# A two-layer decoder trunk on one core: the second layer's compressed keys and norm steps on other engines, and unread products in TensorE's waits

## Chip, core and metric

One core of a Trainium2 chip runs the whole program. The metric is device time in microseconds (us) of one execution; the time before is a median of three runs, 762.18 us (760.72 to 763.38). The engines that matter are TensorE (PE in the profile; PEld is its weight load), VectorE (DVE), ScalarE (ACT), GpSimd (POOL), and SyncE (SP), which issues nearly all transfers.

## What is computed

A trunk of two residual layers over 256 tokens of width 1024, all float32. Cut to what matters:

```
h = x
layer 0: mix = dilated sliding-window attention(h)          # 16 heads, three dilations
layer 1: on its way in, once:
           kv = h @ w_kv                                    # six blocks of 256 columns
           k_cmp, v_cmp = compress(kv[0]), compress(kv[1])  # gelu(blocks @ w1 + b1) @ w2 + b2
         q = h @ w_q + b_q; gates = sigmoid(h @ w_gate + b)
         mix = gate0*attn(q, k_cmp, v_cmp) + gate1*attn(q, k_slc, v_slc) + gate2*attn(q, k_win, v_win)
both:    h = layer_norm(ALPHA*h + mix)
         ffn = 16 experts of width 256, two per token (group router, then expert router)
         h = layer_norm(ALPHA*h + ffn)
layer_norm(x) = (x - mean) * rsqrt(var + eps) * g + b
```

## The kernel before

The program is one long stream without loops on the chip. Token chunks are c = 0 and 1, of 128 rows each. Its stages are: attention of layer 0 (0 to 280 us), output projection and router of layer 0 (280 to 313), the sixteen experts of layer 0 in four rounds (313 to 432), the norm between the layers (432 to 447), the shared keys and values and the compressed ones (447 to 530), attention of layer 1 (530 to 620), router (620 to 634), experts (634 to 748) and the last norm (748 to the end).

*Order.* A list scheduler lays out each engine's instructions ahead of time: of the instructions that are ready in its own model of time it takes the one that stands first in the program, and later ones fill holes. On the chip each engine then goes through its list strictly in that order. Blocks under `tc.manual_schedule(engines=PES)` keep TensorE's instructions in the written order. Weight loads are one queue on SP in a written order (`stream`); each waits for a free buffer.

*PSUM banks.* There are eight: two of tag A, two of S, one each of Y, R, T and O. `banks(A="AAYR", ...)` says which tags the uses A, S, T and O go through in turn; `B(use, ...)` takes the next. `banks(A="AA", S="SSY", T="TR", O="O")` at line 969 sets the turns anew at the start of the shared keys and values.

*Projections.* `split` turns a weight block into a high part `wh` (ScalarE, line 251, four pieces of 128x512) and a low part `wl` (subtraction, line 252, VectorE or the engine in `low`). `projT` and `projN` then make 48 products of 256 columns in one bank (`psT_`, `psN_`): 32 read `wh` and 16 read `wl`. `b_q(g)`, g = 0 to 3, makes the queries of layer 1; for g = 1 and 2 the subtractions are GpSimd's. `stack_q` puts the queries in place, with ScalarE casts (lines 313, 314) and VectorE subtractions (315, 316).

*The norm between the layers* (lines 937 to 960). For each chunk: sum of squares on ScalarE (487); z = (x - mean)*g on VectorE (946); `rstd`, nine VectorE instructions on one column (lines 496 to 506: an add, two scalings, three Newton steps of two); z*y + b (950); eight transposes on TensorE (553); then high part, low part and plain copy out of PSUM (955 on ScalarE, 956 on VectorE, 957 on ScalarE). VectorE's list mixes this with the low parts of two weight blocks. The last norm (1220 to 1234) has the same parts, and some of chunk 0's on GpSimd (1228, 1229).

*Compressed keys and values* (1024 to 1082). `hd` is the hidden layer; `hps` transposes it, `hcT` and `hrep` copy it (1059, 1063). Then

```python
    kc_ps = B("O", [64, 64], "kc_ps")          # keys: two products
    V.tensor_scalar(kcs, kc_ps, b2k[0:64], None, op0=ALU.add)
    for half in range(2):
        vc_ps = B("O", [P, 64], "vc_ps")       # values: three products, same single bank O
        S.copy(vcs, vc_ps)
```

so the first `vc_ps` waits until `kcs` has read `kc_ps`. Then come `b_q(1)` and `gx`, the gate logits: products of 48 columns.

*Router* (`Moe.enter`, `route`). Per chunk: transposes, `lt`, copy `ls` (566), `lg`, a chain of small VectorE instructions to `o12` (584), the rank product `rk`, `pos` (849). `moe_round` then gathers rows: `gps`, 32 products of 256 columns plus four with zeros that open the banks (line 655), and the first expert's products `G`.

Of the kernel before, what the change touches and what calls it, by code (L numbers as in the profile page):

```python
# [132 lines left out]
def layers(tc, A, out, pools, keep, general):  # L133
# [23 lines left out]
    def B(use, shape, name):  # L157
        tag = rot[use][turn[use] % len(rot[use])]
        turn[use] += 1
        return psum[tag].tile(shape, F32, tag=tag, name=name)  # L160
# [325 lines left out]
                continue  # L486
            S.activation(junk, r[:, s], AF.Square, bias=nm, scale=1.0, accum_out=q[:, n : n + 1])

    def rstd(q, y):


        n = y.shape[1]
        vh = sm.tile([P, n], F32, tag="vh", name="vh")
        yi = sm.tile([P, n], I32, tag="yi", name="yi")
        t = sm.tile([P, n], F32, tag="yt", name="yt")
        V.tensor_tensor(vh, q[:, :, 0], q[:, :, 1], op=ALU.add)
        V.tensor_scalar(vh, vh, -0.5 / D, -0.5 * EPS, op0=ALU.mult, op1=ALU.add)
        V.tensor_scalar(yi, vh.bitcast(I32), -0.5, 519526879.0, op0=ALU.mult, op1=ALU.add)
        y0 = yi.bitcast(F32)
        for _ in range(3):  # L500
            if n == 1:
                V.scalar_tensor_tensor(t, y0, vh, y0, op0=ALU.mult, op1=ALU.mult)
            else:
                V.tensor_tensor(t, y0, vh, op=ALU.mult)
                V.tensor_tensor(t, t, y0, op=ALU.mult)
            V.scalar_tensor_tensor(y, t, 1.5, y0, op0=ALU.add, op1=ALU.mult)
            y0 = y


    tri = small[:, 1024:1152]  # L510
# [45 lines left out]
    def route(layer, r, q, y, c, cc, o12, sel):  # L556

        wr = wrs[layer]
        rT = pp.tile([P, 8, P], F32, tag="p", name="rT")
        transposeT(r, lambda g, ps: (V.tensor_copy if g == c == 0 else S.copy)(rT[:, 4 * g : 4 * g + 4], ps))  # L560
        lt = B("T", [P, P], "lt")
        for k in range(8):
            b = 32 * (k % 4)
            mm(lt[b : b + 32], wr[:, k], rT[:, k], k < 4, k >= 4)
        ls = kp.tile([P, P], F32, tag="k", name="ls")
        V.tensor_copy(ls, lt)
        lg = B("O", [P, 24], "lg")
        mm(lg, ls, cst("lsel"), True, True)
        rstd(q.unsqueeze(1), y)
        L = mp.tile([P, 24], F32, tag="L", name="L")  # L570
        V.scalar_tensor_tensor(L, lg, y, brs[:, layer], op0=ALU.mult, op1=ALU.add)
        gm = sm.tile([P, 8], F32, tag="gm", name="gm")
        gi = sm.tile([P, 8], U32, tag="gi", name="gi")
        s4 = sm.tile([P, 4], F32, tag="s4", name="s4")
        V.max(gm, L[:, 0:8])
        V.max_index(gi, gm, L[:, 0:8])
        V.tensor_tensor(s4, cst("io16")[:, 0:4], gi[:, 0:1].to_broadcast([P, 4]), op=ALU.not_equal)
        em = mp.tile([P, 16], F32, tag="em", name="em")
        V.scalar_tensor_tensor(em.rearrange("p (g e) -> p g e", g=4), s4.unsqueeze(2).to_broadcast([P, 4, 4]), NEG, L[:, 8:24].rearrange("p (g e) -> p g e", g=4), op0=ALU.mult, op1=ALU.add)
        ev = sm.tile([P, 8], F32, tag="ev", name="ev")  # L580
        ei = sm.tile([P, 8], U32, tag="ei", name="ei")
        V.max(ev, em)
        V.max_index(ei, ev, em)
        V.tensor_tensor(o12, cst("io16").unsqueeze(1).to_broadcast([P, 2, 16]), ei[:, 0:2].unsqueeze(2).to_broadcast([P, 2, 16]), op=ALU.is_equal)
        V.tensor_add(sel, o12[:, 0], o12[:, 1])

        def weights():

            wt = sm.tile([P, 4], F32, tag="wt", name="wt")
            ex = sm.tile([P, 4], F32, tag="ex", name="ex")  # L590
            V.tensor_scalar(wt[:, 0:1], gm[:, 0:1], -1.0, None, op0=ALU.mult)
            S.activation(ex, L[:, 0:4], AF.Exp, bias=wt[:, 0:1], scale=1.0, accum_out=wt[:, 1:2])
            V.tensor_sub(wt[:, 2:3], ev[:, 1:2], ev[:, 0:1])
            S.activation(wt[:, 2:3], wt[:, 2:3], AF.Exp)
            V.scalar_tensor_tensor(wt[:, 1:2], wt[:, 2:3], 1.0, wt[:, 1:2], op0=ALU.add, op1=ALU.mult)
            V.reciprocal(wt[:, 1:2], wt[:, 1:2])
            V.tensor_mul(wt[:, 3:4], wt[:, 2:3], wt[:, 1:2])
            V.tensor_scalar(cc[:, c], o12[:, 0], wt[:, 1:2], None, op0=ALU.mult)
            V.scalar_tensor_tensor(cc[:, c], o12[:, 1], wt[:, 3:4], cc[:, c], op0=ALU.mult, op1=ALU.add)

        return weights
# [17 lines left out]
    def moe_round(layer, hH, hL, r, sums, pos, cc, hook, late, later, rest):  # L619
# [116 lines left out]
        for qd in range(5):  # L736
# [20 lines left out]
            with tc.manual_schedule(engines=PES):  # L757
                if qd:
                    yH = W(1, [P, 2, D], "yH", F32R)
                    yL = W(2, [P, 2, D], "yL", F32R)  # L760
                    down(2 * qd - 2, ha, yH, yL)
                    down(2 * qd - 1, hb, yH, yL)
                    whole[qd - 1] = (ohT, yH, yL)
                if qd < 4:
                    ga = up(2 * qd, xg)
                    if qd == 0:
                        ohT_, cslots_ = places(C)
                    gb_ = up(2 * qd + 1, xg)
                    whole[qd] = (ga, gb_, ohT_, cslots_)
                else:  # L770
                    scatter(3, *whole.pop(3))

    def moe_rest(layer, hH, hL, r, pos, cc):

# [41 lines left out]
    class Moe:  # L816
# [15 lines left out]
        def enter(self, c):  # L832
# [19 lines left out]
            if c == 0:  # L852
                self.low(0, y)
                self.weights[0]()

        def low(self, c, y):
            u, hH, hL = self.u[c], self.hH, self.hL
# [82 lines left out]
    for c in range(2):  # L940
# [4 lines left out]
        for s in halves:  # L945
            V.scalar_tensor_tensor(z[:, s], x[:, c, s], nm, gb[:, 0, s], op0=ALU.add, op1=ALU.mult)
        y = sm.tile([P, 1], F32, tag="y2", name="y2")
        rstd(q.unsqueeze(1), y)
        for s in halves:
            V.scalar_tensor_tensor(z[:, s], z[:, s], y, gb[:, 1, s], op0=ALU.mult, op1=ALU.add)  # L950

# [4 lines left out]
            V.tensor_tensor(dL, src, dH.bitcast(F32), op=ALU.subtract)  # L956
            S.copy(dT, src)

        transposeT(z, evac, "A")
        zs.append(z)  # L960

    for a in range(4):
# [3 lines left out]
    pre["w"] = split(pre["w"])  # L966


    banks(A="AA", S="SSY", T="TR", O="O")
    st["ahead"] = AH3  # L970
    bm = pre["bm"]
    o = [0]
# [70 lines left out]
    qSt = [U([P, 16, P], "qS", F32R) for c in range(2)]  # L1043

    def b_q(g):
        ps = projT(split(take(("wq", g)), low=nc.gpsimd if g in (1, 2) else V), aH, aL)
        for pr in range(2):
            j = 2 * g + pr
            q = kp.tile([P, T], F32, tag="k", name="q")
            S.activation(q, ps[:, pr], AF.Identity, bias=bqs[:, j : j + 1], scale=cst("qs")[:, j : j + 1])  # L1050
            for c in range(2):
                stack_q(qSt[c], j, q[:, c * P : (c + 1) * P])
# [12 lines left out]
    for f in range(2):  # L1065
        mm(kc_ps, w2[:, 0, f], hcT[:, f, 0:64], f == 0, f == 1)
    kcs = sm.tile([64, 64], F32, tag="kcs", name="kcs")
    V.tensor_scalar(kcs, kc_ps, b2k[0:64], None, op0=ALU.add)
    KC = sm.tile([P, 4, 2, 16], F32R, tag="KC", name="KC", bufs=1)
    kcs4 = kcs.rearrange("p (g n) -> p g n", g=4)  # L1070
    for r_ in (lo, hi):
# [3 lines left out]
    for half in range(2):  # L1075
# [4 lines left out]
        vcs = kp.tile([P, 64], F32, tag="k", name="vcs")  # L1080
        S.copy(vcs, vc_ps)
        nc.gpsimd.tensor_tensor(VC[:, 8 * half : 8 * half + 8], vcs.unsqueeze(1).to_broadcast([P, 8, 64]), hm.unsqueeze(2).to_broadcast([P, 8, 64]), op=ALU.mult)
    b_q(1)

    gx = B("T", [P, 2, 48], "gx")
# [134 lines left out]
    for c in range(2):  # L1220
# [7 lines left out]
                nc.gpsimd.tensor_scalar(h2[:, c, s], h[:, c, s], nm, 1.0, op0=ALU.add, op1=ALU.mult)  # L1228
                nc.gpsimd.tensor_tensor(h2[:, c, s], h2[:, c, s], gb[:, 0, s], op=ALU.mult)
        y = sm.tile([P, 1], F32, tag="y", name="y")  # L1230
        rstd(q.unsqueeze(1), y)
        for s, eng in zip(halves, (nc.sync, S)):
            V.scalar_tensor_tensor(h2[:, c, s], h2[:, c, s], y, gb[:, 1, s], op0=ALU.mult, op1=ALU.add)
            eng.dma_start(out[c][:, s], h2[:, c, s])
# [69 lines left out]
```

## Time and profile before

| | |
|---|---|
| median of 3 runs | 762.18 us |
| the profiled execution: its time, its span | 763.41 us, 761.6 us |
| TensorE busy, mean granted clock | 716.1 us (94%), 0.961 of 2.4 GHz |
| VectorE, ScalarE, GpSimd busy | 409.7 us (54%), 319.4 us (42%), 71.4 us (9%) |
| transfers | 166.84 MB, 219 GB/s mean |

A clock of 1.00 is 2.4 GHz and 0.50 is 1.2 GHz; a figure between them is a stretch with some of each. A busy TensorE is not one at its peak: products are pipelined, and at half clock the same busy time holds half the work.

### The profile page before, as it was taken

What the parts mean: (1) busy time and instruction counts of PE and PEld (TensorE: products, weight loads), DVE (VectorE), ACT (ScalarE), POOL (GpSimd) and SP (SyncE); (2) the same over time, 40 slices, a digit from 0 to 9 for tenths busy, and PEclk for the clock granted to TensorE, in tenths of its full rate; (3) what the DMA queues carried; (4) which work ended last, traced back from release to release, by engine and by line L of the source; (5) the groups of instructions that cost most, each with busy time, mean ns of one, the idle gap of its engine ahead of it and who ended that gap; (6) DMA issues with size and microseconds to landing.
All of it is one profiled execution on the core that took longest, in us unless ns stands there. A gap on an engine that the chain in (4) does not pass through costs nothing. (4 is left out here: it accounts for less than half of the span.)

```text
span 761.6 us, 12692 instructions
## 1 busy us (share of the span) xinstructions
PE 716.1 (94%) x4996; PEld 534.2 (70%) x4996; DVE 409.7 (54%) x1066; ACT 319.4 (42%) x709; POOL 71.4 (9%) x107
## 2 busy tenths in 40 slices
PE   8999999999999998999999669979999979999993
PEld 6999999999999976545353369879766635453541
DVE  4664556467455647552341658544885565331426
ACT  5555545555454534131230554434874421321312
POOL 0000000000000001110100002230233221000101
PEclk9999999999999999799999969987999998999997
DMA  7975343434443355589999950103780057798921
GB/s 265 408 279 194 111 166 117 164 123 153 167 166 112 114 219 214 216 341 422 415 416 420 397 168 1 56 1 119 299 357 1 2 188 288 322 413 358 415 114 61
DMA packets 27221, 166.84 MB, mean 219 GB/s; under 512 B 3720, under 2 KB 4232, under 8 KB 9104
## 3 DMA queue, kind: packets, MB, share of 16 engines
q1 hardware_dynamic: 26720, 165.35, 55.3%
q8 instruction: 41, 0.67, 0.4%
q10 hardware_dynamic: 432, 0.59, 0.2%
q14 instruction: 28, 0.23, 0.1%
HBM read 163.83 MB, written 1.05 MB: 216 GB/s over the span
## 5 line engine op out<-in xcount | busy, mean ns | idle before, releaser
L252 DVE TENSOR_TENSOR wl<-w,wh 128x512 fp32r<-128x512 f32 (+1 forms) x123 | 118.1, 993 | 89.3 <-ACT wh L251 71.3
L251 ACT CAST wh<-w 128x512 fp32r<-128x512 f32 (+1 forms) x131 | 104.1, 843 | 87.9 <-issue 15.7
L167 PE MATMUL G<-w,xg 128*64 128x512 f32 x416 | 92.2, 593 | 0.0
L167 PEld LDWEIGHTS G<-w,xg 128*64 128x64 f32 x416 | 29.7, 137 | 58.1 <-issue 55.5
L167 PE MATMUL Y<-wd,hidT 128*64 128x512 f32 x256 | 57.8, 595 | 0.0
L611 DVE SCALAR_TENSOR_TENSOR sil<-sil,G 128x256 f32<-128x256 f32 x16 | 6.7, 420 | 76.1 <-ACT sil L610 76.1
L167 PEld LDWEIGHTS Y<-wd,hidT 128*64 128x64 f32 x256 | 17.8, 137 | 33.7 <-issue 33.3
L176 DVE TENSOR_TENSOR yL<-Y,yH 128x512 fp32r<-128x512 f32 x32 | 22.1, 692 | 32.5 <-ACT yH L175 32.5
L175 ACT CAST yH<-Y 128x512 fp32r<-128x512 f32 x32 | 18.8, 586 | 36.5 <-PE Y L167 36.5
L1150 ACT ACTIVATE p<-p,nmb 128x128 f32<-128x128 f32 (+1 forms) x64 | 28.5, 447 | 10.1 <-DVE nmb L1149 10.1
L616 ACT COPY hidT<-ht 128x256 f32<-128x256 f32 x16 | 6.0, 373 | 63.6 <-PE ht L615 63.6
L167 PE MATMUL gps<-oh,hH 128*128 128x256 f32 x128 | 30.7, 323 | 0.8 <-DVE kept L862 0.8
L167 PE MATMUL mix<-w,obT 128*128 128x512 f32 x64 | 31.1, 601 | 0.0
L167 PE MATMUL gps<-oh,hL 128*128 128x256 f32 x128 | 29.3, 310 | 0.0
L1159 POOL TENSOR_SCALAR p<-p,lb,gates 128x256 f32<-128x256 f32 (+1 forms) x40 | 22.3, 566 | 67.3 <-ACT p L1150 34.4
L610 ACT ACTIVATE sil<-G 128x256 f32<-128x256 f32 x16 | 6.2, 387 | 52.3 <-PE G L167 52.3
L730 DVE SCALAR_TENSOR_TENSOR x<-x,sps 128x512 f32<-128x512 f32 x32 | 21.8, 684 | 11.2 <-PE sps L167 11.0
L167 PE MATMUL sps<-yH,ohT 128*128 128x512 f32 x64 | 25.9, 405 | 0.0
L405 ACT ACTIVATE p<-p,nm 128x384 f32<-128x384 f32 x32 | 19.6, 614 | 14.2 <-DVE nm L404 14.2
L167 PE MATMUL sps<-yL,ohT 128*128 128x512 f32 x64 | 25.3, 396 | 0.0
L167 PEld LDWEIGHTS gps<-oh,hH 128*128 128x128 f32 x128 | 23.7, 225 | 1.8 <-issue 1.5
L648 ACT ACTIVATE xg<-gps,lnT 128x256 f32<-128x256 f32 x32 | 16.1, 562 | 19.5 <-PE gps L167 18.8
(558 smaller groups left out, 1796.7 us busy)
## 6 DMA issues: line engine op xcount, KB each, us to landing
w<-in_gu SPq DMA_DIRECT2D x52, 1024.0 KB, 10.7
w<-in_a_win SPq DMA_DIRECT2D x35, 1024.0 KB, 5.9
wd<-in_dn SPq DMA_DIRECT2D x32, 1024.0 KB, 9.5
wp<-in_gu SPq DMA_DIRECT2D x24, 512.0 KB, 13.2
w<-in_wkv SPq DMA_DIRECT2D x6, 1024.0 KB, 16.6
w<-in_a_wout SPq DMA_DIRECT2D x4, 1024.0 KB, 4.7
w<-in_w SPq DMA_DIRECT2D x4, 1024.0 KB, 19.9
w<-in_wq SPq DMA_DIRECT2D x4, 1024.0 KB, 4.7
```

Source lines behind the costliest of these rows:

```text
L167: nc.tensor.matmul(out, l, r, start=start, stop=stop)
L175: S.copy(dstH, src)
L176: V.tensor_tensor(dstL, src, dstH.bitcast(F32), op=ALU.subtract)
L251: S.copy(h[:, s], w[:, s])
L252: low.tensor_tensor(l[:, s], w[:, s], h[:, s].bitcast(F32), op=ALU.subtract)
L405: S.activation(w, w, AF.Exp, bias=nm, scale=-1.0, accum_out=l)
L610: S.activation(sil[rows], G[:, 0:256], AF.Tanh, scale=0.5)
L611: V.scalar_tensor_tensor(sil[rows], sil[rows], 1.0, G[:, 0:256], op0=ALU.add, op1=ALU.mult)
L648: S.activation(xg[:, k], banks4[k // 2][:, k % 2], AF.Identity, bias=b_, scale=g_)
L730: V.scalar_tensor_tensor(r[:, c, s], r[:, c, s], 1.0 if qd else ALPHA, ps, op0=ALU.mult, op1=ALU.add, accum_out=sums[:, c, n : n + 1])
L1150: S.activation(dst, dst, AF.Exp, bias=nm[:, hl, b : b + 1], scale=-1.0, accum_out=l[:, hl, b : b + 1])
L1159: eng.tensor_scalar(dst, dst, l[:, hl, b : b + 1], gates[:, c, 1 + b, 4 * g + hl : 4 * g + hl + 1], op0=ALU.mult, op1=ALU.mult)
```

## The change

`rstd` takes an engine, and its first Newton instruction becomes a `tensor_scalar` with two column operands; chunk 0 of the norm between the layers and of the last norm gives it GpSimd. A new function `awake` issues products into a bank of use S that nobody reads: 38 of 512 columns after layer 0's last expert products, 9 after chunk 1's transposes in the norm, and in each of both routers two times 6 of 128 columns in float32, on `ls` of chunk 0 and of chunk 1. The transposes of the norm go under manual order. The call of `banks` moves from the start of the shared keys and values to just ahead of `b_q(1)`, so until there the turns of layer 0's experts hold (A="AAYR", S="S", T="T", O="O"). The low parts of `b_q(1)` and `b_q(2)` go to VectorE, and `kcs` to ScalarE.

```diff
-    def rstd(q, y):
+    def rstd(q, y, eng=V):
...
         for _ in range(3):
-            if n == 1:
-                V.scalar_tensor_tensor(t, y0, vh, y0, op0=ALU.mult, op1=ALU.mult)
+            eng.tensor_scalar(t, y0, vh, y0, op0=ALU.mult, op1=ALU.mult)
+            eng.tensor_scalar(y, t, 1.5, y0, op0=ALU.add, op1=ALU.mult)
+            y0 = y
+
+    def awake(n, l=None):
+
+        ps = B("S", [P, 512], "idle")
+        for _ in range(n):
+            if l is None:
+                mm(ps, ones, small[:, 0:512], True, True)
             else:
...
+                mm(ps[:, 0:P], l, l, True, True)
...
         V.tensor_copy(ls, lt)
+        st["ls", c] = ls
...
                     scatter(3, *whole.pop(3))
+                    if layer == 0:
+                        awake(38)
...
                 self.weights[0]()
+            else:
+                for n in range(2):
+                    awake(6, st["ls", n])
...
-        rstd(q.unsqueeze(1), y)
+        rstd(q.unsqueeze(1), y, V if c else nc.gpsimd)
...
-        transposeT(z, evac, "A")
+        with tc.manual_schedule(engines=PES):
+            transposeT(z, evac, "A")
+            if c:
+                awake(9)
...
-    banks(A="AA", S="SSY", T="TR", O="O")
     st["ahead"] = AH3
...
-        ps = projT(split(take(("wq", g)), low=nc.gpsimd if g in (1, 2) else V), aH, aL)
+        ps = projT(split(take(("wq", g))), aH, aL)
...
-    V.tensor_scalar(kcs, kc_ps, b2k[0:64], None, op0=ALU.add)
+    S.activation(kcs, kc_ps, AF.Identity, bias=b2k[0:64], scale=1.0)
...
+    banks(A="AA", S="SSY", T="TR", O="O")
     b_q(1)
...
-        rstd(q.unsqueeze(1), y)
+        rstd(q.unsqueeze(1), y, V if c else nc.gpsimd)
```

## Rows read from the trace of the kernel before

**Rows 1.** TensorE's waits: what waited for what, us in total, times, longest.

```profile
PE hps L553 <- DVE z L950: 9.9, 2, 9.4
...
PE vc_ps L167 <- DVE kcs L1068: 3.8, 1, 3.8
...
PE psT__4818 L167 <- ACT VV L1021: 1.7, 1, 1.7
```

**Rows 2.** Stretches: length, busy and count by engine, TensorE's granted clock, transfers.

```profile
core 0: us, PE busy (x) PEld busy (x) DVE busy (x) ACT busy (x) POOL busy (x), PEclk, DMA share, GB/s
...
302.00:308.00 6.00, 5.04 (x36) 4.50 (x37) 4.11 (x32) 2.13 (x6) 0.61 (x1) 0.55 1.02 427
...
447.00:453.00 6.00, 5.86 (x28) 5.81 (x29) 2.21 (x2) 4.14 (x5) 0.00 (x0) 0.52 0.62 209
...
627.30:633.00 5.70, 5.67 (x25) 5.17 (x25) 4.56 (x12) 0.00 (x0) 1.05 (x1) 0.50 1.01 372
```

**Rows 3.** Timeline of the norm between the layers: start, us, engine, line, operation.

```profile
434.50 0.19 ACT L487 ACTIVATION_READ_ACCUMULATOR junk<-x,nmean 128x1 f32 x1
...
440.86 1.41 DVE L950 SCALAR_TENSOR_TENSOR z<-z,y,lngb 128x512 f32<-128x512 f32 x2
...
447.14 0.58 PE L167 MATMUL psT__4534<-hTH,wh 128*128 128x256 f32 x1 [1.91 <-ACT hTH L955]
```

**Rows 4.** Timeline: runs of like products, with zeros, at full and at half clock.

```profile
297.17 0.81 PE L167 MATMUL gps<-small,zero 1*128 1x512 bf16 x3
...
454.54 2.08 PE L167 MATMUL psT__4534<-hTH,wl 128*128 128x256 f32 x16
...
513.06 3.62 PE L167 MATMUL psT__5104<-hTH,wl 128*128 128x256 f32 x16
```

**Rows 5.** The chain that ended last, 503 to 531 us: start, us, what.

```profile
503.48 1.27 DVE qS L315
...
506.05 0.28 DVE qS L315
...
508.29 1.73 PE vc_ps L167 x6
...
510.96 1.36 PE vc_ps L167 x6
512.32 4.35 PE psT__5104 L167 x19
516.67 5.09 PE gx L167 x36
521.76 8.62 PE psT__5211 L167 x48
```

**Rows 6.** Timeline of GpSimd and ScalarE at the compressed keys.

```profile
500.71 5.16 POOL L252 TENSOR_TENSOR wl<-w,wh 128x512 fp32r<-128x512 f32 x4 [6.25 <-ACT wh L251]
...
503.98 0.30 ACT L314 CAST qS<-q 64x128 fp32r<-64x128 f32 x1
```

**Rows 7.** Two stretches of 1 us in and after the gate logits.

```profile
520.00:521.00 1.00, 1.00 (x11) 1.00 (x10) 0.57 (x2) 0.15 (x1) 0.00 (x0) 1.00 0.02 8
521.00:522.00 1.00, 1.00 (x5) 0.83 (x5) 0.00 (x0) 0.20 (x1) 0.00 (x0) 0.50 0.00 0
```

**Rows 8.** GpSimd's groups by shape: count, busy us, mean ns, idle before.

```profile
L1159 POOL TENSOR_SCALAR p<-p,lb,gates 128x128 f32<-128x128 f32 x16 | 8.1, 515 | 38.9 <-ACT p L1150 27.2 <-DVE nmb L1149 7.1 <-PE ptb L1168 3.0
...
L1294 POOL MEMSET const-float32-0.0<- 128x1 f32 x1 | 0.1, 99 | 0.2 <-issue 0.2
```

**Rows 9.** Timeline of the second router, VectorE.

```profile
627.10 0.17 DVE L849 SCALAR_TENSOR_TENSOR pos<-rk,sel 128x16 f32<-128x16 f32 x1
```

**Rows 10.** The chain that ended last, at the second router.

```profile
627.33 7.13 PE gps L167 x33
```

**Rows 11.** Timeline: the first expert of layer 0.

```profile
313.08 7.09 PE L167 MATMUL G<-w,xg 128*64 128x512 f32 x32
```

**Rows 12.** Timeline of the last norm, GpSimd and VectorE.

```profile
748.62 1.57 POOL L1229 TENSOR_TENSOR h<-h,lngb 128x512 f32<-128x512 f32 x1
...
753.17 1.41 DVE L1233 SCALAR_TENSOR_TENSOR h<-h,y,lngb 128x512 f32<-128x512 f32 x2
```

More of the change, by code (lines that the diff above doesn't have):

```diff
@@ L487, in squares @@
             S.activation(junk, r[:, s], AF.Square, bias=nm, scale=1.0, accum_out=q[:, n : n + 1])
-    def rstd(q, y):
[L492 to L498, printed above, removed]
+    def rstd(q, y, eng=V):
+        vh = sm.tile([P, 1], F32, tag="vh", name="vh")
+        yi = sm.tile([P, 1], I32, tag="yi", name="yi")
+        t = sm.tile([P, 1], F32, tag="yt", name="yt")
+        eng.tensor_tensor(vh, q[:, 0, 0:1], q[:, 0, 1:2], op=ALU.add)
+        eng.tensor_scalar(vh, vh, -0.5 / D, -0.5 * EPS, op0=ALU.mult, op1=ALU.add)
+        eng.tensor_scalar(yi, vh.bitcast(I32), -0.5, 519526879.0, op0=ALU.mult, op1=ALU.add)
         y0 = yi.bitcast(F32)
         for _ in range(3):
-            if n == 1:
-                V.scalar_tensor_tensor(t, y0, vh, y0, op0=ALU.mult, op1=ALU.mult)
-            else:
[L504 to L507, printed above, removed]
+            eng.tensor_scalar(t, y0, vh, y0, op0=ALU.mult, op1=ALU.mult)
[6 more added lines that the diff above has]
+                mm(ps, ones, small[:, 0:512], True, True)
+            else:
+                mm(ps[:, 0:P], l, l, True, True)
     tri = small[:, 1024:1152]
```

## The prediction

> **What bounds the kernel now.** I read the table of engines first: TensorE is busy for 94% of the span, so time can come only from its waits or from its clock. Next its list of waits [rows 1]: three matter here, 9.4 us for the normed rows `z`, 3.8 us of `vc_ps` for `kcs`, and 1.7 us for a free bank. Then the granted clock by stretches [rows 2]: after each long wait the same products go on at 0.50 to 0.55, that is at 1.2 GHz, while the busy column looks full. The price of half clock is in two runs of sixteen like products: 2.08 us at 2.4 GHz and 3.62 us at 1.2 GHz, which is 0.12 us and 0.21 us for each once the last one's own duration is taken off [rows 4]. So a wait is paid twice, as idle time and as slow products behind it. The chain that ended last shows it at its plainest: TensorE idles until 508.29 and works without a hole to 530.38, mostly at half speed [rows 5].
>
> **The change part by part.** The sum is made against the profiled execution, 763.41 us; the median of the runs lies 1.2 us below it.
>
> *The compressed keys.* Before, the wait begins at 508.29 - 3.8 = 504.5, and the last product of `psT__5211` ends at 521.76 + 8.62 = 530.4: 25.9 us [rows 1, 5]. `kcs` came last on VectorE because GpSimd's four subtractions ran from 500.71 to 505.87 [rows 6] and VectorE's subtraction of 64x128 took 1.27 us beside them and 0.28 us after [rows 5]. The Trainium skill's SBUF — State Buffer, section "Who interferes with whom", says that a VectorE instruction with two SBUF inputs and a GpSimd one that reads SBUF block each other fully; by that rule, the trace agrees, 1.27 against 0.28. After, the subtractions are VectorE's: eight more, at most GpSimd's 1.29 us each [rows 6], hidden in VectorE's idle time ahead of the hidden layer and beside TensorE's products; without that cover the four of `b_q(2)` would cost up to 5 us. `kcs` is one ScalarE instruction of about 0.3 us (VectorE's took as much). In front of it stand at worst ScalarE's eight casts, the last of which ends at 504.28 [rows 6], so it ends by 504.6, while TensorE still has 22 products of `psT__5104` to fill the wait. What is left then: 22 at 0.12 = 2.6; the two `vc_ps` groups 3.1 now, between half of that and all, say 2.0; `gx`, 36 products at the 10 to 11 per us that the window at full clock shows [rows 7], 3.4; `psT__5211`. Does the clock hold for it? In the window from 520 `gx` runs at 1.00 with TensorE busy throughout, and from 521 the clock is 0.50, with no idle time between [rows 7]: all that TensorE did ahead of the fall was `gx`. I take that to happen again and leave `psT__5211` at its 8.6. Sum 16.6, and 0.5 for small waits: 17.1, a gain of **8.8 us**. Bounds: 0 if the wait stays, 11.6 if `psT__5211` runs at full clock (48 at 0.12 = 5.8).
>
> *The norm between the layers.* The nine instructions of chunk 0 start at 434.7, when its squares are done, and its `z` came at 440.86 [rows 3]. GpSimd's price for one column has no row; its nearest are 0.10 for a MEMSET of one column and 0.515 for a TENSOR_SCALAR of 128 columns [rows 8]. I take 0.4 to 0.5, near the second, because it is the same operation with column operands: 434.7 + 4 = 438.7 (bounds 435.6 and 439.3). The 38 unread products are 0.21 us each by the distance of the three with zeros [rows 4], 8.1 us. They start when TensorE falls idle, 9.4 us ahead of the first transpose, which follows the first of the two `z` instructions at 441.7 [rows 1, 3], so at 432.3, and end at 440.4: the transposes start 1.3 us earlier and with the clock up. VectorE's list loses nine small instructions and gains dearer forms of others; I cost that at nothing, hidden under its weight subtractions. The first projection began at 447.14 [rows 3], and in 447 to 453 TensorE did 28 products where 50 fit at 0.12 [rows 2]: 2.6 us. Against that stand the nine unread products, 1.9 us, in front of the projection; most of it is hidden, for the last high parts come late from ScalarE's queue of eight copies. Together **2.0 us**, bounds 0 and 3.
>
> *Banks.* With four A banks the 1.7 us wait [rows 1] loses its bank half; the weights of that projection are split in the same queues just then, so I take **0.8 us** of 0 to 1.7.
>
> *Second router.* The 33 gather products take 7.13 us from 627.33 [rows 10], 25 of them in 5.7 us at 0.50 [rows 2]; at 0.12 they take 4.0. The unread products are 24 records, at 0.10 to 0.26 us each (`gx` and `vc_ps` are the nearest), 2.4 to 6.2 us in a stretch with some 3 us idle. A second effect: the last zero product waited for the bank R, held by `rk` until `pos` read it at 627.10 [rows 9, 10]. With `hps` of the hidden layer asked for before `banks` instead of after, the turns of T and R swap by one and `rk` gets T, so chunk 0's gather can start while VectorE works out chunk 1's rank. 3.1 plus 0.4: **3.5 us**, bounds 0 and 4.7.
>
> *First router.* The same at a smaller size: 302 to 308 at 0.55 [rows 2]. Chunk 1's sixteen products would save about 1 us until `G` at 313.08 [rows 11], and `lt` and `lg` ahead of the chain 0.5: **1.5 us**, bounds 0 and 2.5. The transfers of the experts wait there for buffers that `G` frees, so they move along.
>
> *Last norm.* GpSimd's nine instructions stand behind its product that ends at 748.62 + 1.57 = 750.2 [rows 12]; at 0.4 to 0.5 they end near 754.2, when before the output rows started at 753.17. Chunk 1's chain has VectorE to itself meanwhile. I take **0**, bounds 0.7 lost and 0.7 won.
>
> Sum: 8.8 + 2.0 + 0.8 + 3.5 + 1.5 = 16.6. 763.41 - 16.6 = 746.8, and 1.2 lower on the scale of the median: **746 us**. The attention of layer 1, where I see only the same list shifted by one bank, can go 2 us either way.
>
> **The rivals.**
>
> *The clock holds through the gate logits.* With no idle wait ahead of them, `gx` is shorter and has wide products on both sides. Then `psT__5211` gives 2.8 us more: 743. Against it speaks the fall at 521 [rows 7]. The Trainium skill's TensorE: Matmul & The Clock Gate, section "Why this matters for your kernels", asks for no idle gaps between bursts of matmuls; by that rule this would be the likeliest, but the row shows a fall with no gap.
>
> *The fillers are too thin.* Between chunk 0's and chunk 1's transposes TensorE may stand still for 2 to 3 us after the 38, and the routers' fillers come when `ls` is there. If the clock falls all the same, the norm and the first router give nothing and the second 1.0 (its bank): 8.8 + 0.8 + 1.0 = 10.6, 752. For it: in the second router the clock fell after a stretch that was sparse, not empty.
>
> *The wait at the compressed keys moves.* The list may put `kcs` behind casts of the next weights, or the new subtractions ahead of `hrep`; then `vc_ps` waits as long as now, and the change gives 7.8: 754.
>
> *Slower: GpSimd's instructions are dear.* Both chains of nine stand at the head of VectorE's list (`z`, the output rows). At X each, the norm is late by 9X - 6.2 and the end by 9X - 3.0 [rows 3, 12]; 18X - 9.2 exceeds the other 14.6 from X = 1.32 us. The longest GpSimd row shown beside a busy VectorE, 1.57 us but for 512 columns and two inputs [rows 12], would give 19.1 lost: 767. Against: 0.515 for 128 columns, also beside a busy VectorE [rows 8]. By the rule of SBUF — State Buffer cited above (the Trainium skill) each of them could also wait for the VectorE instruction then running; no row here shows that for one column.
>
> **How the numbers follow.** Forecast 0.45; clock holds 0.20; fillers too thin 0.22; wait moves 0.07; slower 0.04; no difference 0.02. The range has to reach from a bit under all good ends (11.6 + 3 + 1.7 + 4.7 + 2.5 + 0.7 = 24.2, 738) to between the last two gains: 738 to 754. 0.3% of this time is 2.3 us, about what can be told from no change. Faster 0.94, same 0.02, slower 0.04.
>
> **What would show it.** In the profile after: no wait of `vc_ps` near 4 us, and `kcs` on ScalarE under 0.4; `gx` at 1.00 and the first half of `psT__5211` at 0.50; 38 products 0.21 apart and transposes at 1.00; first projection at 0.12 a product; the second router's gather starting before its last `pos`, 32 products in about 4 us; GpSimd's nine at 0.4 to 0.5. Wrong it would be if one-column GpSimd work took over 1 us, if the unread products ran 0.43 apart, or if a new wait of several us stood in layer 1's attention.

## The result, and the profile of the changed kernel

The changed kernel takes 753.12 us (median of five runs, 750.46 to 754.13) against 762.18 us for the kernel before: the ratio is 0.987 with a 95% interval from 0.986 to 0.989. It is faster, by 9.1 us where 16 were forecast. The profiled execution is the quickest of the five (750.46 us, span 748.7, mean clock 0.987); the other four have a mean clock of 0.982. Against the profiled execution of before (span 761.6) it gained 12.9 us. Both gaps, from 16 to 12.9 and from 12.9 to 9.1, have to be explained.

I cut the span at five places that every profile shows: the end of layer 0's last expert product, the end of the compressed hidden layer `hd`, the first compressed score `cmp`, the first expert product of layer 1, the end of its last one. Each entry is the length between two of them in us; the fifth stretch, the experts of layer 1, is 114.0 in all but one (114.2 in e4). The runs e1 to e11 are the experiments below.

| kernel | median us | ratio to before | start to last expert product, layer 0 | norm, projections, `hd` | compressed keys | attention, second router | last norm |
|---|---|---|---|---|---|---|---|
| before | 762.18 | | 432.3 | 62.4 | 35.6 | 104.2 | 13.2 |
| changed | 753.12 | 0.987 | 429.8 | 62.5 | 25.6 | 101.0 | 15.8 |
| e1 both norms on VectorE | 749.71 | 0.983 | 431.4 | 61.4 | 27.1 | 101.1 | 13.3 |
| e2 chunk 1's chain first | 746.42 | 0.980 | 429.7 | 58.4 | 27.0 | 101.2 | 13.9 |
| e3 last norm on VectorE | 751.58 | 0.986 | 429.4 | 63.5 | 28.5 | 100.9 | 13.3 |
| e4 no idle products | 757.47 | 0.993 | 432.5 | 64.0 | 28.5 | 102.5 | 15.7 |
| e5 gate logits split | 751.24 | 0.985 | 430.3 | 63.7 | 24.5 | 101.8 | 15.7 |
| e6 best of both | 744.25 | 0.977 | 430.4 | 59.0 | 24.5 | 101.6 | 12.8 |
| e7 compressed keys alone | 753.27 | 0.988 | 430.8 | 62.4 | 27.0 | 103.5 | 12.8 |
| e8 banks alone | 759.53 | 0.996 | 432.1 | 59.0 | 34.5 | 102.7 | 13.3 |
| e9 norm ordered by hand | 742.71 | 0.975 | 430.6 | 57.2 | 24.5 | 101.7 | 12.9 |
| e10 e2 without 38 and 9 | 747.33 | 0.981 | 431.1 | 60.5 | 25.6 | 101.0 | 13.3 |
| e11 chunk 1 on GpSimd | 750.52 | 0.985 | 430.8 | 61.3 | 28.5 | 101.0 | 14.6 |

The first two lines show the changed kernel at once: 2.5 us won before the norm, 10.0 at the compressed keys, 3.2 behind them; nothing in the stretch that holds the norm, and 2.6 lost at the last norm. One profile's stretch is not exact: with the same instructions, e11 and e5 have 430.8 and 430.3 us to the last expert product, and e3 and e5 63.5 and 63.7 us in the norm's stretch.

The norm between the layers, GpSimd, VectorE and TensorE of the changed kernel (start, length, engine, line, operation; in brackets the idle time and who ended it), which answers to [rows 3]:

```profile
432.34 0.59 POOL L495 TENSOR_TENSOR vh<-sq 128x1 f32<-128x1 f32 x1 [57.45 <-ACT junk L487]
433.02 1.17 POOL L496 TENSOR_SCALAR vh<-vh 128x1 f32<-128x1 f32 x1
434.26 0.19 POOL L497 TENSOR_SCALAR yi<-vh 128x1 int32<-128x1 int32 x1
434.56 0.34 POOL L500 TENSOR_SCALAR yt<-yi,vh 128x1 f32<-128x1 f32 x1
...
436.82 0.27 POOL L501 TENSOR_SCALAR y<-yt,y 128x1 f32<-128x1 f32 x1
```

```profile
433.45 0.68 DVE L252 TENSOR_TENSOR wl<-w,wh 128x512 fp32r<-128x512 f32 x1
437.12 1.41 DVE L960 SCALAR_TENSOR_TENSOR z<-z,y,lngb 128x512 f32<-128x512 f32 x2 [2.99 <-POOL y L501]
438.45 0.15 DVE L495 TENSOR_TENSOR vh<-sq 128x1 f32<-128x1 f32 x1
...
441.35 0.68 DVE L252 TENSOR_TENSOR wl<-w,wh 128x512 fp32r<-128x512 f32 x1
...
442.74 2.00 DVE L966 TENSOR_TENSOR hTL<-hps,hTH 128x512 fp32r<-128x512 f32 x2
444.65 0.21 DVE L501 TENSOR_SCALAR y<-yt,y 128x1 f32<-128x1 f32 x1
...
445.45 1.42 DVE L960 SCALAR_TENSOR_TENSOR z<-z,y,lngb 128x512 f32<-128x512 f32 x2
```

```profile
429.67 8.38 PE L167 MATMUL idle<-small,ones 128*128 128x512 bf16 x38
437.93 1.32 PE L557 MATMUL hps<-cs,z 128*128 128x128 f32 x8
446.25 1.97 PE L557 MATMUL hps<-cs,z 128*128 128x128 f32 x8 [7.01 <-DVE z L960]
448.02 2.64 PE L167 MATMUL idle<-small,ones 128*128 128x512 bf16 x9
```

GpSimd is done 4.8 us after it began (4 were forecast), and chunk 0's transposes start early and at full clock. But VectorE stands idle for 3.0 us with chunk 1's whole chain behind the instruction that waits: its first step is at 438.45, its last just before 445.45. Between these steps stand six weight subtractions of 0.68 us, which could have filled the idle time, and chunk 0's low parts (2.0 us). TensorE, which had one wait of 9.4 us for `z`, now has one of 7.0 us between the two chunks. The clock falls there: the 442 to 449 window shows 0.52 (columns as in [rows 2]).

```profile
436.00:442.00 6.00, 3.24 (x18) 1.57 (x16) 4.88 (x13) 2.00 (x2) 0.88 (x4) 1.00 0.14 36
442.00:449.00 7.00, 2.75 (x11) 2.12 (x12) 5.24 (x11) 3.61 (x4) 0.15 (x1) 0.52 0.98 342
```

The last norm, VectorE, beside [rows 12], has the same picture: idle for 3.1 us in front of chunk 0's output, with the rest of chunk 1's first part and its nine steps behind, so that chunk 1's output starts 4.2 us after chunk 0's (2.0 us before: 753.17 [rows 12], 755.14).

```profile
738.28 1.41 DVE L1246 SCALAR_TENSOR_TENSOR h<-h,y,lngb 128x512 f32<-128x512 f32 x2 [3.08 <-POOL y L501]
739.62 0.74 DVE L1239 SCALAR_TENSOR_TENSOR h<-x,nmean,lngb 128x512 f32<-128x512 f32 x1
740.28 0.15 DVE L495 TENSOR_TENSOR vh<-sq 128x1 f32<-128x1 f32 x1
...
742.27 0.21 DVE L501 TENSOR_SCALAR y<-yt,y 128x1 f32<-128x1 f32 x1
742.52 1.42 DVE L1246 SCALAR_TENSOR_TENSOR h<-h,y,lngb 128x512 f32<-128x512 f32 x2
```

The compressed keys, TensorE, answering to [rows 5]: `vc_ps` waits 0.8 us instead of 3.8, now for `hrep`, which stands behind eight subtractions of 64x128 on VectorE; `kcs` is on ScalarE from 501.99 to 502.30, behind its eight casts.

```profile
503.00 0.41 PE L167 MATMUL vc_ps<-bm,hrep 128*128 128x64 f32 x2 [0.77 <-DVE hrep L1075]
...
507.61 1.88 PE L167 MATMUL gx<-bm,hT 128*128 128x48 f32 x16
...
511.69 0.42 PE L167 MATMUL gx<-bm,ones 1*128 1x48 f32 x2
517.89 0.96 PE L167 MATMUL cmp<-KC,qS 128*128 128x32 f32 x8
```

In this execution the clock stays at 1.00 through `gx` and the projection behind it. The second router: the gather of chunk 0 now begins before chunk 1's ranks (`rk`), and its 32 products take 4.3 us to the first `G` where before took 6.6 (the 7.1 of [rows 10] count one product with zeros more).

```profile
612.40 1.58 PE L167 MATMUL idle<-ls 128*128 128x128 f32 x12
...
614.56 0.39 PE L167 MATMUL gps<-oh,hH 128*128 128x256 f32 x1
614.78 0.28 PE L167 MATMUL gps<-oh,hL 128*128 128x256 f32 x1
614.90 0.21 PE L167 MATMUL rk<-o,small 128*128 128x16 bf16 x2
...
618.87 1.08 PE L167 MATMUL G<-w,xg 128*64 128x512 f32 x4
```

### The profile page after: what moved, and what is told of

It reads as the page before. It is cut to its first block, busy times and chain, and to the rows that moved or that the text cites. A ratio compares the mean times of both kernels' runs of the same rounds, so it can differ in the third digit from the quotient of the medians.

```text
span 748.7 us, 12880 instructions
## 1 busy us (share of the span) xinstructions
PE 715.0 (95%) x5091; PEld 528.4 (71%) x5091; DVE 411.1 (55%) x1055; ACT 319.3 (43%) x710; POOL 68.4 (9%) x117
## 4 chain that ended last, share of the span: by engine, by line
PE 87%; DVE 6%; ACT 2%; POOL 1%; issue 1%; DMA 1%; SPq 0%; POOLq 0%; DVEq 0%; ACTq 0%
PE G L167 15%; PE Y L167 7%; PE mix L167 6%; PE po L167 5%; PE gps L167 4%; PE sps L167 3%; PE sc L167 3%; PE ptb L1181 2%; PE s L167 2%; PE pt L420 2%; ACT wh L251 1%; PE psN__665 L167 1%; PE psN__2959 L167 1%; PE psN__2186 L167 1%; PE psN__1419 L167 1%
## 5 line engine op out<-in xcount | busy, mean ns | idle before, releaser
L252 DVE TENSOR_TENSOR wl<-w,wh 128x512 fp32r<-128x512 f32 (+1 forms) x131 | 123.2, 974 | 86.1 <-ACT wh L251 78.5
L1163 ACT ACTIVATE p<-p,nmb 128x128 f32<-128x128 f32 (+1 forms) x64 | 28.5, 448 | 8.2 <-DVE nmb L1162 7.9
L735 DVE SCALAR_TENSOR_TENSOR x<-x,sps 128x512 f32<-128x512 f32 x32 | 21.8, 684 | 15.0 <-PE sps L167 14.6
L167 PE MATMUL gps<-oh,hH 128*128 128x256 f32 x128 | 26.5, 290 | 0.1
L167 PE MATMUL gps<-oh,hL 128*128 128x256 f32 x128 | 26.0, 285 | 0.2 <-DVE hL L869 0.2
L167 PE MATMUL sps<-yH,ohT 128*128 128x512 f32 x64 | 25.9, 405 | 0.0
L167 PE MATMUL G<-wp,xg 128*64 128x512 f32 x96 | 23.7, 594 | 0.0
```

Source lines behind the costliest of these rows:

```text
L167: nc.tensor.matmul(out, l, r, start=start, stop=stop)
L252: low.tensor_tensor(l[:, s], w[:, s], h[:, s].bitcast(F32), op=ALU.subtract)
L735: V.scalar_tensor_tensor(r[:, c, s], r[:, c, s], 1.0 if qd else ALPHA, ps, op0=ALU.mult, op1=ALU.add, accum_out=sums[:, c, n : n + 1])
L1163: S.activation(dst, dst, AF.Exp, bias=nm[:, hl, b : b + 1], scale=-1.0, accum_out=l[:, hl, b : b + 1])
```

## Experiments

**e1, both norms on VectorE.** Is it GpSimd's part that lost the norms' time?

```diff
-rstd(q.unsqueeze(1), y, V if c else nc.gpsimd)
+rstd(q.unsqueeze(1), y)
```

> The changed kernel with both norms' nine-instruction chains of chunk 0 back on VectorE; all the rest as changed. Theory (list order): with GpSimd computing chunk 0's chain, VectorE waits for it with chunk 1's chain queued behind, which cost 2.9 us at the norm between the layers and 2.6 us at the last norm. Then this kernel is about 5.5 us under the changed one (4 to 7): some 747.5 us, ratio to the kernel before 0.980; the third projection starts some 3 us sooner after the last expert products than the 32.3 us of the changed kernel, and the span ends about 13.2 us after the last expert products instead of 15.8. Rival (the idle products and the clock, not GpSimd, lost the norm's time): the norm keeps its 32.3 us, only the last norm may gain; 750.5 us or more, ratio 0.984 or more.

749.71 us, 3.4 under the changed kernel, less than the 4 to 7 expected. The last norm gave its 2.5 us. At the norm the stretch came down only by 1.1 us against the profile of the changed kernel and by 2.1 against that of e3, whose norm is the same. So GpSimd's part did lose time at both places, but VectorE alone, in the list that the scheduler makes, loses some there too: chunk 1's steps lie between weight subtractions, and its transposes start 14.1 us after the last expert product.

**e2, the same work on the same engines, another order.** The order of VectorE's list is written by hand at both norms.

```diff
+    with tc.manual_schedule(engines=VES):
+        for c in range(2):
...
+            rstd(q.unsqueeze(1), y, V if c else nc.gpsimd)
...
-        for s in halves:
-            V.scalar_tensor_tensor(z[:, s], z[:, s], y, gb[:, 1, s], op0=ALU.mult, op1=ALU.add)
+        for c in range(2):
+            for s in halves:
+                V.scalar_tensor_tensor(zs[c][:, s], zs[c][:, s], ys[c], gb[:, 1, s], op0=ALU.mult, op1=ALU.add)
```

> The changed kernel with GpSimd still computing chunk 0's chain at both norms, but VectorE's list written by hand so that chunk 1's nine instructions stand ahead of the multiplications that wait for GpSimd. Theory (list order): the loss was chunk 1's work queued behind the wait, so nearly all of it comes back: about 5 us under the changed kernel (3.5 to 6), some 748 us, ratio 0.981; at the last norm h of chunk 1 follows h of chunk 0 with no chain between. Rival (GpSimd's chain itself is too long): chunk 0's multiplication still starts 4.8 us and 3.6 us after the squares, and the time falls by under 1 us: 752 us or more.

746.42 us (744.40 to 749.83 over six runs), ratio 0.980 (0.977 to 0.983): 6.7 us, more than the 3.5 to 6 expected, and 3.3 us under e1 by the medians, though the two intervals overlap. All sixteen transposes now come as one run, 10.8 us after the last expert product; the clock does not fall at the norm. The order of the list was the cause. Three things in it changed at once, and no run separates them: chunk 1's chain stands ahead of the wait, the weight subtractions fill the time of the wait, and chunk 0's low parts come after chunk 1's `z`. One thing differs from the expectation: chunk 0's `z` still waits for GpSimd (0.63 us), for now VectorE is busy beside it, and GpSimd's chain takes 7.5 us instead of 4.8:

```profile
432.20 0.59 POOL L496 TENSOR_TENSOR vh<-sq 128x1 f32<-128x1 f32 x1 [58.36 <-ACT junk L488]
432.88 1.78 POOL L497 TENSOR_SCALAR vh<-vh 128x1 f32<-128x1 f32 x1
434.74 0.58 POOL L498 TENSOR_SCALAR yi<-vh 128x1 int32<-128x1 int32 x1
435.43 1.30 POOL L501 TENSOR_SCALAR yt<-yi,vh 128x1 f32<-128x1 f32 x1
436.84 0.68 POOL L502 TENSOR_SCALAR y<-yt,yi 128x1 f32<-128x1 f32 x1
...
439.42 0.27 POOL L502 TENSOR_SCALAR y<-yt,y 128x1 f32<-128x1 f32 x1
```

```profile
439.72 2.74 DVE L966 SCALAR_TENSOR_TENSOR z<-z,y,lngb 128x512 f32<-128x512 f32 x4 [0.63 <-POOL y L502]
440.53 2.65 PE L558 MATMUL hps<-cs,z 128*128 128x128 f32 x16 [2.62 <-DVE z L966]
```

At the last norm the order brings most of the loss back, not all: 13.9 us against 13.3 with the chain on VectorE (e1, e3).

**e3, the last norm alone.** The first edit of e1, at the last norm only.

> The changed kernel with the last norm's chain of chunk 0 back on VectorE alone. List order: 2.6 us under the changed kernel (2.0 to 3.0), about 750.5 us, the end 13.2 us after the last expert products instead of 15.8. Rival (the end hangs on the output's DMAs or the first half from GpSimd): the end stays 15 us or more after the last expert products, and the time at 753 us.

The end comes 13.3 us after the last expert product, 2.5 us sooner, as expected. The time, 751.58 us, is only 1.5 us under the changed kernel by the medians; e3's own profile shows why a median here says less than a stretch: in it the clock falls at the end of the gate logits (512 on), where the changed kernel's profile held 1.00.

```profile
509.00:512.00 3.00, 3.00 (x27) 2.89 (x26) 2.78 (x9) 2.72 (x10) 0.00 (x0) 1.00 0.00 0
512.00:519.00 7.00, 7.00 (x34) 6.82 (x34) 2.68 (x8) 1.39 (x3) 0.00 (x0) 0.51 0.43 153
```

**e4, no idle products.** The three calls of `awake` are taken out.

```diff
-awake(38)
...
-awake(6, st["ls", n])
...
-awake(9)
```

> The changed kernel without any of the products that nobody reads (38 and 9 at the norm, 6 and 6 at each router). Theory: they earned the routers' time, 2.6 us before the first expert products and about 3 us in the second router, and nothing at the norm, where the clock fell nevertheless: about 5.5 us over the changed kernel (4 to 7), 758.5 us, ratio 0.995. Rival (the routers' gain came from elsewhere in the change, the products are idle in both senses): within 1 us of the changed kernel, 753 us.

757.47 us, 4.4 over the changed kernel: they earn about a half of the 9.1. Where they earn it the stretches say less surely: 2.7 us before the norm, 1.5 in the second router, 1.5 in the norm's stretch. Only the second is clear of what stretches with the same instructions vary by: before the norm e7, without these products, has the 430.8 of e11, which has them, and the norm's 64.0 is 0.3 over e5's 63.7. The 3 us at the compressed keys are the clock after the gate logits, where no such product stands in either kernel. The second router without them still does the gather of chunk 0 ahead of the ranks and is 1.7 us shorter than before; then its clock falls to half.

**e5, the gate logits in two runs.** Is the clock after `gx` the reason for the four other runs at 0.982? `gate(c)` holds the 18 products of chunk c; the tile `gx` moves to a bank of S.

```diff
+    with tc.manual_schedule(engines=PES):
+        for f in range(2):
+            nc.tensor.transpose(hps[:, f], hs[:, f * P : (f + 1) * P], ident)
+        gate(0)
...
     b_q(1)
-    for c in range(2):
-        for k in range(8):
-            mm(gx[:, c], hT[:, k, c * P : (c + 1) * P], wgt[:, k], k == 0, False)
-        mm(gx[:, c], ones1[32:33], brow[32:33, 0:48], False, True)
+    gate(1)
```

> The changed kernel with the 36 narrow products of the gate logits in two runs: chunk 0's 18 straight after the two transposes of the compressed hidden layer, chunk 1's 18 where all 36 stood; one projection of 48 products (256 columns each) lies between. Theory: in most runs of the changed kernel the clock still falls to half at the end of those 36 narrow products (clock 0.982 where the profiled run has 0.987, some 7 us of half clock more, that is 2 to 3.5 us), and that is why the median gained 9.1 us and the profiled run 12.9. With no more than 18 narrow products in one run the clock stays at 1.00 from the norm to the last experts, every run comes out near the profiled 750.5 us, and the spread shrinks: 750.5 us (749.5 to 751.5), ratio 0.984. Rival (the missing 0.005 of clock lies at the norm or the end): the split changes nothing, 753 us, and the profile shows no fall here in either.

751.24 us; every run has a mean clock of 0.986 to 0.988. The compressed keys take 24.5 us, and TensorE's clock is 1.00 through all of them:

```profile
502.00:510.00 8.00, 8.00 (x62) 7.47 (x63) 4.17 (x14) 4.00 (x14) 2.09 (x2) 1.00 0.00 0
510.00:512.00 2.00, 2.00 (x20) 2.00 (x19) 1.23 (x3) 1.71 (x5) 0.00 (x0) 1.00 0.03 8
```

The stretch to the second router grew by 0.8 us: chunk 1's ranks (615.53) stand ahead of chunk 0's gather (616.30) again, as in before, and so they do in e6 and e9. The likely reason is that `gx`, now in a bank of S, no longer takes a turn of T, which shifts the bank of `rk`; no run tests it. The table fits that reading of the spread: the compressed keys are 25.6 us where the clock held (changed, e10), 27.0 where it fell for a part of the next projection (e1, e2, e7), 28.5 where it fell for most of it (e3, e4, e11). Of eight such profiles with `gx` in one run and `kcs` on ScalarE, six show the fall.

**e6, the best of both.** e2's order at the norm between the layers, e3's last norm, e5's split, and the Newton steps on VectorE in their old form.

```diff
+            if eng is V:
+                V.scalar_tensor_tensor(t, y0, vh, y0, op0=ALU.mult, op1=ALU.mult)
+                V.scalar_tensor_tensor(y, t, 1.5, y0, op0=ALU.add, op1=ALU.mult)
+            else:
...
```

> The changed kernel with chunk 1's chain written ahead of chunk 0's multiplication at the norm between the layers, the last norm's chain on VectorE again, the two Newton steps on VectorE in their old form (scalar_tensor_tensor, 0.22 and 0.16 us in the routers of before against 0.27 and 0.21 us of tensor_scalar after), and the gate logits split. If the four add up: 4.9 us at the norm as in the run with chunk 1's chain first, 2.5 us at the end as with the last norm on VectorE, 0.3 us in each router, and 2 to 3 us of clock: about 10 us under the changed kernel, 743 us (741 to 746), ratio 0.974. Rival (what the norm gains, the clock or the first projections give back): 746.5 us or more.

744.25 us, ratio 0.977 (0.975 to 0.979): 8.9 us under the changed kernel. The parts add up nearly: 3.5 us in the norm's stretch, 1.1 at the compressed keys against the held clock and 4.0 against the fallen, 3.0 at the end.

**e7 and e8, two terms of the sum by themselves, from the kernel before.**

```diff
-split(take(("wq", g)), low=nc.gpsimd if g in (1, 2) else V)
+split(take(("wq", g)))
...
-V.tensor_scalar(kcs, kc_ps, b2k[0:64], None, op0=ALU.add)
+S.activation(kcs, kc_ps, AF.Identity, bias=b2k[0:64], scale=1.0)
```

> The kernel before with two edits alone: the sum of the compressed keys on ScalarE, and the low parts of query projections 1 and 2 on VectorE instead of GpSimd. The prediction's term for them is 8.8 us, with a clock that falls again after the gate logits: 753.5 us (752 to 755), ratio 0.988. If the clock holds through the gate logits as in the profiled run of the changed kernel, 10 to 11.6 us: 751.5 us. Rival (part of the stage's 10 us came from the banks or the shorter wait ahead of it): 5 us or less, 757 us or more.

753.27 us against 762.04 for the runs of before beside it: 8.8 us, the predicted term (7.5 to 10.8 by the interval). In its profile the clock falls after `gx`, as predicted, but for 3.4 us (512.7 to 516.2) where it fell for 6.8 before. So these two lines alone give what the whole change gives by the medians; which of the two gives it no run separates.

```diff
-    banks(A="AA", S="SSY", T="TR", O="O")
     st["ahead"] = AH3
...
+    banks(A="AA", S="SSY", T="TR", O="O")
     b_q(1)
```

> The kernel before with one edit alone: the PSUM banks of the second layer are dealt out anew behind the compressed keys instead of ahead of the first projection. Theory: it gives the 2.6 us of the stretch from the third projection to the first query projection (the prediction had 0.8), and, by another order of TensorE's list in the second router (chunk 0's gathering products ahead of chunk 1's ranks), up to 1.7 us there: 758.5 us (757.5 to 760), ratio 0.9945. Rival (the prediction's own size): 0.8 to 1.2 us, 761 us; the 2.6 us would then belong to the idle products.

759.53 us, ratio 0.996 (0.995 to 0.998): 2.5 us. The 1.7 us wait for `VV` [rows 1] is gone and `hd` is one run of 64 products; and TensorE's list in the second router has chunk 0's gather ahead of chunk 1's ranks, as in the changed kernel, with no idle product:

```profile
620.42 0.39 PE L167 MATMUL gps<-oh,hH 128*128 128x256 f32 x1
...
623.40 0.26 PE L167 MATMUL rk<-o,small 128*128 128x16 bf16 x2
```

The profile gains 3.4 us in the norm's stretch, 1.1 at the compressed keys and 1.5 to the second router, more than the median does, and gives 2.4 us back in layer 0's first experts (121.6 us from the first expert product to the last, 119.2 before), which these edits do not touch; that part varies between the runs.

**e9, the norm ordered by hand, without GpSimd.** From e6; `rstd_steps` yields the nine instructions one by one, and the transposes with their evacuations and the splitting of the first weight stand, in this order, in the same hand-written block.

```diff
-            rstd(q.unsqueeze(1), y, V if c else nc.gpsimd)
+            steps.append(rstd_steps(q.unsqueeze(1), y))
+        for _ in zip(*steps):
+            pass
```

> The best kernel so far with no chain on GpSimd: at the norm between the layers VectorE computes both chains, their steps alternating, then the four multiplications z, then the low parts of the transposed rows, and only then the weight subtractions, all in a list written by hand. Theory: in the runs with chunk 1's chain first, GpSimd's nine instructions took 6.7 to 7.7 us from first to last instead of 4.8, because VectorE's weight subtractions ran beside them (0.58 to 1.78 us each for 0.19 to 0.34), so z waited for GpSimd after all; eighteen steps on VectorE alone are 18 times some 0.14 us, 2.5 us, z starts 6.4 us after the last expert products instead of 10.2, and the first projection some 13.5 us after them instead of 17.1: 3 us under the best kernel (2 to 4), 741 us, ratio 0.973. Rival (the weight subtractions moved behind the norm are late for the projections): 744 us or more, with waits of the projections for low parts.

742.71 us, ratio 0.975 (0.973 to 0.977), 10.4 us under the changed kernel and 1.5 under e6, where the two intervals overlap. The eighteen steps take 2.1 us on VectorE, two of a kind in 0.27 to 0.38 us:

```profile
433.85 0.38 DVE L496 TENSOR_TENSOR vh<-sq 128x1 f32<-128x1 f32 x2
434.15 0.27 DVE L497 TENSOR_SCALAR vh<-vh 128x1 f32<-128x1 f32 x2
...
435.69 0.28 DVE L502 SCALAR_TENSOR_TENSOR y<-yt,y 128x1 f32<-128x1 f32 x2
435.95 2.74 DVE L972 SCALAR_TENSOR_TENSOR z<-z,y,lngb 128x512 f32<-128x512 f32 x4
```

TensorE waits for no `z` any more; the first projection starts 12.7 us after the last expert product (17.1 in e6, 14.9 before). Of that, 2.6 us went back: TensorE now waits 0.9 us for a weight's low part and 0.5 us for a low part of the transposed rows, the two projections in question take 7.6 and 7.0 us where e6 has 5.9 and 6.0, and it needs 44.5 us to the end of `hd` where e6 needs 41.9. The rival was right in kind and too high in size.

**e10, e2 without the 38 and the 9.**

> The kernel with chunk 1's chain first at both norms (the run e2), without the 38 and the 9 products that nobody reads at the norm between the layers; those of the routers stay. If they hold the clock once the wait is short: the clock falls in the norm's wait for 7 to 17 us (7 us in the changed kernel, 17 us before), the 16 transposes and part of the first projection run at half rate, and the time is 3 to 5 us over e2's 746.4: 750 us, ratio 0.985. Rival (they are worth nothing, as between the changed kernel and the run without any of them, where the norm took 18.4 and 18.9 us): 746.5 us, ratio 0.980.

747.33 us, ratio 0.981 (0.978 to 0.984), against 0.980 (0.977 to 0.983): not told apart. The profile does show the clock falling in the norm's wait, and the norm's stretch 2.1 us longer than e2's. That the idle products at the norm earn something is likely from the stretch and not shown by the time.

**e11, the chunks exchanged.**

```diff
-rstd(q.unsqueeze(1), y, V if c else nc.gpsimd)
+rstd(q.unsqueeze(1), y, nc.gpsimd if c else V)
```

> The changed kernel with the two chunks exchanged: at both norms VectorE computes chunk 0's chain and GpSimd chunk 1's. List order: the instruction that waits for GpSimd now has nothing of weight behind it, and GpSimd's chain runs beside chunk 0's multiplications, so most of the 5 us comes back: about 748.5 us (747 to 750.5), ratio 0.981 to 0.984. Rival (GpSimd's chain itself is too long, 6 us and more beside VectorE's weight subtractions): z of chunk 1 starts no sooner than the 445.4 of the changed kernel, 752 us or more.

750.52 us, ratio 0.985 (0.983 to 0.987), between the two expectations. At the norm the low parts of chunk 0, which wait for ScalarE, stand ahead of chunk 1's `z` (444.54, though GpSimd ended at 441.96). At the end the order has the same fault again: an output of chunk 1 that waits for GpSimd stands ahead of chunk 0's last step.

```profile
740.12 0.27 DVE L500 TENSOR_SCALAR yt<-y,vh 128x1 f32<-128x1 f32 x1
742.43 0.75 DVE L1246 SCALAR_TENSOR_TENSOR h<-h,y,lngb 128x512 f32<-128x512 f32 x1 [2.04 <-POOL y L501]
743.10 0.21 DVE L501 TENSOR_SCALAR y<-yt,y 128x1 f32<-128x1 f32 x1
743.22 2.07 DVE L1246 SCALAR_TENSOR_TENSOR h<-h,y,lngb 128x512 f32<-128x512 f32 x3
```

## Why the prediction was right, and where it failed

**The direction and the main term held.** The size did not: 753.1 us lies one us inside the range's upper end, 9.1 us won where 16 were forecast. The compressed keys were to give 8.8 us with a falling clock: e7 measured 8.8 in time. That the two agree to the digit is luck. From the start of the wait to the end of the projection behind `gx` the forecast was 17.1 us, and e7's profile has 17.3 (503.1 to 520.4); but `gx` takes 4.6 us there where I had 3.4, for the 10 to 11 products per us that I read from one window [rows 7] are not the rate of all 36 (8 per us in the changed kernel at full clock), and the projection takes 7.4 where I had 8.6, for the fall was half as long. With a fall of 6.8 us (e3) the same stretch takes 18.8 us, with none (the changed kernel's profile) 15.8. Of the 25.9 us the term is thus worth 7.1 to 10.1, by the clock, and its upper bound of 11.6 was too high mostly by the same `gx`. The profile of the changed kernel shows 10.0, because there the rival "the clock holds through the gate logits" came true. It is the exception, as the forecast had it: in the other four runs the mean clock is 0.005 lower, which over 750 us is twice 3.8, 7.5 us more at half clock, the size of the fall that e3's windows show. Of the 3.9 us between the profiled runs' gain (12.95) and the medians' (9.06), 1.2 is that before's profiled run stands above its median, and 2.7 that the changed kernel's stands under its own. That these 2.7 are the clock at `gx` rests on e5, where that fall is prevented and all runs lie at 750.0 to 751.9; none of the four other runs has a profile.

**The step that failed** is the norms: "VectorE's list loses nine small instructions … I cost that at nothing", and at the end "Chunk 1's chain has VectorE to itself meanwhile. I take 0". The price of GpSimd's steps was about right (4.8 us for 4, with one step of 1.17 us beside VectorE's work). What was wrong is that VectorE has nothing "meanwhile": it takes its list in order, and the scheduler had put chunk 0's multiplication ahead of chunk 1's chain and of the weight subtractions between its steps. Instead of 2.0 and 0 won, the last norm lost 2.6 us (13.2 to 15.8; e3 gets them back), and the norm between the layers about 3.5: its stretch stayed at 62.4 and 62.5 although the banks alone bring it to 59.0 (e8). That is some 8 us under the forecast. The profile's 12.9 against the sum of 16.6 then comes out to 0.1: 5.5 less at the norm and 2.6 less at the last norm, 2.6 more from the banks (3.4 in that stretch, for 0.8), 1.2 more at the compressed keys, 1.0 more ahead of the norm, 0.3 less in the second router. The slower rival had the place right, "both chains of nine stand at the head of VectorE's list", and the price wrong: by its 9X - 6.2, X = 0.53 still wins 1.4 us. It counted how long VectorE waits and not what waits behind it. e2, with the same instructions on the same engines, shows that the order cost it, but for 0.6 us at the last norm (13.9 against 13.3).

**"The fillers are too thin"** was right about the gap between the chunks' transposes: the clock did fall there. But it was a wait of 7.0 us, not of 2 to 3, and the routers' fillers did hold: the clock is 1.00 in both routers in all nine profiles that have them, and falls in both in all four without (before, e4, e7, e8). Its time, 752, is nearer to the measured 753.1 than the forecast's, by luck: it had the norm at nothing, which lost 3.5 us, and the routers at 1.0, which gave more.

**Terms that were mis-sized.** The banks, 0.8 and 0.4 in the second router, gave 2.5 by the medians (e8; 1.8 to 4.0 by the interval). In the second router 3.5 was forecast and 3.2 came, but as some 1.7 (e4; 1.5 in e8) for the gather that no longer waits for the ranks and 1.5 for the clock, where I had 0.4 and 3.1. The first router, 1.5, came to 2.5 at the end of layer 0. How much of that the idle products earn is open: without them the first expert product starts at 312.8 (e4), but before's own list gave 310.4 and 311.7 (e8, e7) as well as 313.1 [rows 11], since the clock falls there for a different time in each profile (10.3 us in before, 10.2 in e4, 6.8 in e7, 3.4 in e8). The attention of layer 1, taken as 0, is 0 within 0.1 us.

## What to carry to other kernels

Moving a short chain to a free engine takes it off the busy engine's time but puts a wait into its list; look up what the scheduler has placed behind that wait before counting anything as hidden, and order the list by hand (independent work first, the waiting instruction last) if it matters. A wait that is paid twice, idle and then at half clock, can be worth more than all its neighbours: two lines at the compressed keys gave as much as the whole change, whose other gains the norms ate up. When the profiled execution is the quickest of its runs, compare mean clocks before building on its stretches.

## What the runs showed of the hardware that was not expected

One-column steps on GpSimd took 0.19 to 0.34 us while VectorE stood idle (the changed kernel, from 434.26 on) and 0.58 to 1.78 us while VectorE ran its 128x512 weight subtractions (e2). The prediction had no row for that. The Trainium skill's SBUF — State Buffer, section "Who interferes with whom", says that the ports shared by VectorE and GpSimd are an exclusive lock, and that a VectorE instruction with two SBUF inputs contends with a GpSimd one that reads SBUF. The trace agrees: beside subtractions of 0.68 us the same step takes 0.58 for 0.19 us (`yi`), 1.30 and 0.70 for 0.34 (`yt`), 0.68 for 0.27 (`y`).

TensorE's clock fell in the last 0.4 to 1.5 us of `gx` with no idle time in the 8 us ahead of it: TensorE was busy throughout, last with the 36 products of 48 columns in one run. It did so in six of eight profiles that are alike there. Two runs of 18 with a projection between them did not make it fall in any profile (e5, e6, e9).

One column of a Newton step on VectorE took 0.27 and 0.21 us as TENSOR_SCALAR with column operands (last norm of the changed kernel and of e11) against 0.22 and 0.16 us as SCALAR_TENSOR_TENSOR (last norm of before), 0.3 us for six steps. Its worth by itself was not measured.
